# Attention of layer 2 in groups of four query blocks, with the causal mask and the row maximum in one VectorE operation

## The chip, the cores and the metric

The kernel runs on one core of a Trainium2 chip. The metric is the time of one execution on the device, in microseconds; a kernel's time is the median of its runs. The engines are named as in the profile: PE is TensorE (PEld its weight loads), DVE VectorE, ACT ScalarE, POOL GpSimd, and SP issues the DMAs.

## What is computed

The reference is a decoder trunk of two layers over 1024 tokens of width 1024. Layer 1 has a stick-breaking attention and a sliding-window attention side by side, layer 2 a multi-head latent attention with 16 heads; each is followed by a SwiGLU feed-forward part, and norms stand ahead of every part. The change lies in the attention of layer 2:

```python
def one_block(args):
    qn_blk, qr_blk, i = args
    s = (jnp.einsum('bqhd,bshd->bhqs', qn_blk, k_nope, preferred_element_type=F32)
         + jnp.einsum('bqhr,bsr->bhqs', qr_blk, k_rope, preferred_element_type=F32)) * scale
    q_pos = i * BLOCK + jnp.arange(BLOCK)
    s = jnp.where(key_pos[None, :] <= q_pos[:, None], s, -jnp.inf)
    p = jax.nn.softmax(s, axis=-1)
    return jnp.einsum('bhqs,bshd->bqhd', p.astype(v.dtype), v)
```

A head has 64 + 32 features for queries and keys (plain and rotary) and 64 for values. Queries attend to themselves and to all earlier tokens.

## The kernel before

**Tiling.** Tokens lie in reverse order, in eight blocks of 128; so query block b attends to the key blocks b to 7, and block b itself is the diagonal one, with a triangular mask. A head has 36 pairs of a query and a key block. Every product that needs more than one pass of TensorE takes its operands as a high and a low part (`hi`, `lo`): scores take three matmuls (high by high, high by low, low by high), and the product of weights and values (PV) takes two, one for each part of the transposed weights, against values that hold both of their parts side by side.

**Order of work.** The 16 heads are worked in 8 pairs p. `steps(p)` gives a list of steps, each with a `score` and a `pv` half, and `drive` strings the steps of all pairs together: the scores of a step are emitted ahead of the previous step's PV, and the projections of the next pair (queries, keys, values: six items and one of DMAs) are spread as filler over the gaps between a pair's steps. The kernel is built under a planner which then fixes the order on each engine from the dependences and its own estimate of times, so instructions of neighbouring steps are mixed.

**A step** is a head h and a pair c of query blocks (2c and 2c + 1), eight steps per head pair. The order is c = 3, 2, 1, 0 for each head; in pair 0 both heads do c = 3, 2 first, since the projections of that pair are done one token half after the other.

**Scores** (L1257 to L1294). A row of a query block is n = 1024 - 128 b wide. It is cut into one or two parts (`cuts`), the diagonal part first; each part goes to a PSUM bank `z`, of which there are three. The three matmuls stand at L1277. For the first part a fourth matmul (L1280), identity by `maskb` in bf16, adds the mask. VectorE takes the negated maximum of each part (L1283), and, where there are two parts, the smaller of the two (L1286). ScalarE then computes Exp with that as its bias (L1290) into a tile `w` and the row's sum. `w` is a ring of four tiles of 1024 columns, which were the trigonometric tables of the rotary part before.

**PV** (`pv`, L347 to L377). Two key blocks by two query blocks are transposed by TensorE into one PSUM bank `t` of 512 columns (L361); where a key block lies ahead of a query block, zeros are put there by a bf16 matmul (L359). ScalarE copies the high part (`pth`, L364), VectorE subtracts to get the low one (`ptl`, L365), and two matmuls of 256 columns per key block accumulate into a PSUM bank `mm` (L369). At the end ScalarE copies half of the rows (L374) and VectorE adds them to the other half into the output tile of a token half (L376). There are three banks for `t`, two for `mm`; the projections use `mm` too.

**After a token half** of a head pair, `normalise` turns the sums into reciprocals, brings them through DRAM to all partitions and multiplies on POOL, and `spill` writes both parts of the result to DRAM.

Of the kernel before, what the change touches and what calls it, by code (L numbers as in the profile page):

```python
# [10 lines left out]
F32 = mybir.dt.float32  # L11
# [9 lines left out]
P = 128  # L21
# [42 lines left out]
class Kernel:  # L64
# [19 lines left out]
    def tl(self, pool, shape, dt, tag, bufs=1):  # L84
        """A tile of a pool, or the next one of the tag's ring."""
# [18 lines left out]
    def consts(self):  # L104
# [4 lines left out]
        self.identb = self.tl(cp, [P, P], BF16, "identb")  # L109
# [12 lines left out]
        self.maskb = self.tl(cp, [P, 2, P], BF16, "maskb")  # L122
        nc.gpsimd.memset(self.maskb, 0.0)
        for i, op in enumerate((ALU.is_gt, ALU.is_ge)):
            nc.gpsimd.affine_select(
                out=self.maskb[:, i, :], in_=self.maskb[:, i, :], pattern=[[1, P]],
                compare_op=op, fill=NEG, base=0, channel_multiplier=-1)
# [18 lines left out]
    def stream(self, units):  # L146
        """Weight units in the order of their use, each loaded one use ahead."""
# [85 lines left out]
    def stat_acc(self, accs, src, k):  # L233
        """Sums of squares: even terms on one engine, odd ones on another."""
# [48 lines left out]
    def spill(self, k, hf, o):  # L283
        """Both parts of a finished head pair to DRAM, where the output projection fetches them."""
# [7 lines left out]
    def normalise(self, sums, hf, o, tag, bufs):  # L292
        """o, rows by head pair and columns by query, over the sums [query, (head, block)] of its rows."""
# [258 lines left out]
    def sb_steps(self, p, boxes, done):  # L552
# [4 lines left out]
        def score(h, c):  # L557
# [5 lines left out]
            for qi in range(2):  # L563
# [4 lines left out]
                for w in cuts:  # L568
# [8 lines left out]
                    if prev is None:  # L577
                        nc.tensor.matmul(z[:, ext:ext + P], self.identb, self.maskb[:, 0, :], start=False, stop=True)
# [946 lines left out]
```

## Time and profile before

| | us |
|---|---|
| median of three runs | 2531.31 (2531.25 to 2532.11) |
| span of the profiled execution | 2526.1 |
| first scores of layer 2 | 1329.65 |
| last PV matmul of layer 2 | 1730.25 |
| granted clock, mean over the span | 0.976 |

The span is the time from the first to the last instruction of one execution that was profiled; the median is of other runs, without a profile, and holds what lies around the span too. The profile gives busy time per engine and per group of instructions, the idle time ahead of a group with what ended it, and the granted clock of TensorE. The chain of work that ended last covers only the last few per cent of the span, so the middle of the kernel is read from stretches of time and from groups by line.

### The profile page before, as it was taken

What the parts mean: (1) busy time and instruction counts of PE and PEld (TensorE: products, weight loads), DVE (VectorE), ACT (ScalarE), POOL (GpSimd) and SP (SyncE); (2) the same over time, 40 slices, a digit from 0 to 9 for tenths busy, and PEclk for the clock granted to TensorE, in tenths of its full rate; (3) what the DMA queues carried; (4) which work ended last, traced back from release to release, by engine and by line L of the source; (5) the groups of instructions that cost most, each with busy time, mean ns of one, the idle gap of its engine ahead of it and who ended that gap; (6) DMA issues with size and microseconds to landing.
All of it is one profiled execution on the core that took longest, in us unless ns stands there. A gap on an engine that the chain in (4) does not pass through costs nothing. (4 is left out here: it accounts for less than half of the span.)

```text
span 2526.1 us, 34111 instructions
## 1 busy us (share of the span) xinstructions
PE 2365.6 (94%) x11364; PEld 1920.4 (76%) x11364; DVE 1960.4 (78%) x2952; ACT 1272.7 (50%) x2571; POOL 975.6 (39%) x761
## 2 busy tenths in 40 slices
PE   7999899997999999999988999999979999999996
PEld 5777678775888888778766888887758888887784
DVE  6988967668766666898987788885597666678988
ACT  6666656544333333444655787774433333344453
POOL 5322233216965343432222323321064344334333
PEclk9999999988999999999999999999989999999998
DMA  3001115741233224653343111135213233255531
GB/s 122 22 34 43 50 60 178 243 164 42 88 121 121 92 105 148 208 174 105 117 132 101 49 63 60 55 133 191 90 42 113 96 109 108 97 173 178 167 102 70
DMA packets 154445, 275.59 MB, mean 109 GB/s; under 512 B 19260, under 2 KB 27933, under 8 KB 154269
## 3 DMA queue, kind: packets, MB, share of 16 engines
q1 hardware_dynamic: 154268, 273.42, 32.1%
q8 instruction: 89, 1.46, 0.2%
q14 instruction: 88, 0.71, 0.1%
HBM read 197.75 MB, written 75.07 MB: 108 GB/s over the span
## 5 line engine op out<-in xcount | busy, mean ns | idle before, releaser
L139 ACT CAST whi<-wa 128x512 fp32r<-128x512 f32 (+1 forms) x438 | 265.9, 608 | 509.7 <-PE mm L217 128.9
L140 DVE TENSOR_TENSOR wlo<-wa,whi 128x512 fp32r<-128x512 f32 (+1 forms) x438 | 332.1, 759 | 70.7 <-ACT whi L139 70.2
L170 POOL TENSOR_TENSOR wa<-s,wa 128x512 f32<-128x512 f32 (+1 forms) x64 | 96.8, 1512 | 357.2 <-DVE wlo L140 330.5
L365 DVE TENSOR_TENSOR ptl<-t,pth 128x512 fp32r<-128x512 f32 x240 | 161.9, 681 | 15.5 <-ACT pth L364 14.4
L140 DVE TENSOR_TENSOR wlo<-wb,whi 128x512 fp32r<-128x512 f32 (+1 forms) x128 | 134.2, 1048 | 38.6 <-ACT whi L139 38.4
L199 POOL TENSOR_TENSOR s<-wb,wb 128x512 f32<-128x512 f32 (+1 forms) x64 | 106.6, 1666 | 144.9 <-DVE wlo L140 136.5
L1277 PE MATMUL z<-mk,mq 128*128 128x512 f32 (+2 forms) x576 | 147.3, 366 | 10.4 <-ACT w L1290 9.7
L361 PE MATMUL t<-ident,w 128*128 128x128 f32 x864 | 145.1, 281 | 10.2 <-DVE ptl L365 6.6
L364 ACT CAST pth<-t 128x512 fp32r<-128x512 f32 x240 | 137.5, 593 | 23.7 <-PE t L361 13.6
L139 ACT CAST whi<-wb 128x512 fp32r<-128x512 f32 (+1 forms) x128 | 77.5, 605 | 139.6 <-PE d L217 44.3
L369 PE MATMUL mm<-pth,v 128*128 128x256 f32 x480 | 140.1, 309 | 4.0 <-ACT pth L364 2.7
L369 PE MATMUL mm<-ptl,v 128*128 128x256 f32 x480 | 132.3, 300 | 9.1 <-DVE ptl L365 8.8
L216 PE MATMUL mm<-hh,whi 128*128 128x512 f32 x312 | 126.3, 405 | 4.8 <-DVE ev L424 2.8
L1290 ACT ACTIVATE w<-z,st 128x512 f32<-128x512 f32 (+3 forms) x192 | 110.6, 582 | 32.8 <-DVE st L1286 23.5
L1283 DVE TENSOR_REDUCE st<-z 128x1 f32<-128x512 f32 (+1 forms) x192 | 104.3, 549 | 27.2 <-PE z L1277 19.1
L218 PE MATMUL mm<-hh,wlo 128*128 128x512 f32 x312 | 122.8, 394 | 0.0
L217 PE MATMUL mm<-hl,whi 128*128 128x512 f32 x312 | 122.7, 393 | 0.0
L170 POOL TENSOR_TENSOR wa<-wa,wa 128x512 f32<-128x512 f32 (+1 forms) x64 | 93.2, 1457 | 66.3 <-issue 52.9
L770 POOL TENSOR_TENSOR c<-c,c 128x512 f32<-128x512 f32 x60 | 91.6, 1539 | 68.9 <-DVE c L865 67.3
L361 PEld LDWEIGHTS t<-ident,w 128*128 128x128 f32 x864 | 103.3, 144 | 18.9 <-DVE ptl L365 7.7
L170 POOL TENSOR_TENSOR wb<-wa,wb 128x512 f32<-128x512 f32 (+1 forms) x64 | 97.4, 1522 | 42.4 <-DMA wa<-w_gate 35.6
L1277 PEld LDWEIGHTS z<-mk,mq 128*128 128x128 f32 x576 | 92.5, 192 | 23.7 <-ACT w L1290 14.9
(507 smaller groups left out, 7532.2 us busy)
## 6 DMA issues: line engine op xcount, KB each, us to landing
ld<-a SPq DMA_DIRECT2D x158, 256.0 KB, 3.7
a<-c SPq DMA_DIRECT2D x120, 256.0 KB, 2.1
wa<-w_gate SPq DMA_DIRECT2D x56, 256.0 KB, 2.6
wa<-w_up SPq DMA_DIRECT2D x56, 256.0 KB, 2.6
wb<-w_gate SPq DMA_DIRECT2D x40, 256.0 KB, 2.8
wb<-w_up SPq DMA_DIRECT2D x40, 256.0 KB, 2.7
wa<-w_in SPq DMA_DIRECT2D x36, 256.0 KB, 2.6
wa<-w_out SPq DMA_DIRECT2D x32, 256.0 KB, 3.5
```

The source lines that it names most:

```text
L139: nc.scalar.copy(hi[:, :n], raw[:, :n])
L140: nc.vector.tensor_tensor(lo[:, :n], raw[:, :n], f(hi[:, :n]), ALU.subtract)
L170: sub = lambda o, x, y: nc.gpsimd.tensor_tensor(o, x, y, ALU.subtract)
L216: mm(ps, wh, xh, start=first, stop=False)
L217: mm(ps, wh, xl, start=False, stop=False)
L218: mm(ps, wl, xh, start=False, stop=last)
L361: nc.tensor.transpose(dst, blocks(qi, kk), self.ident)
L364: nc.scalar.copy(hi, t)
L365: nc.vector.tensor_tensor(lo, t, f(hi), ALU.subtract)
L369: nc.tensor.matmul(o[:, :256], vs, pt[:, j * 256:(j + 1) * 256], start=(kb == kb0 and j == 0 and i == 0), stop=(kb == NB - 2 and j == 1 an ...
L1277: nc.tensor.matmul(z[:, :wd + ext], qq[:, q0:q0 + P], kk[:, k0 - ext:k0 + wd], start=y == 0, stop=y == 2 and x > 0)
L1290: nc.scalar.activation(w[:, o:o + wd], zs[x], AF.Exp, bias=st[:, 2 * np_ - 2:2 * np_ - 1], accum_out=box[p]["s"][c // 2][:, 8 * x + j:8 * ...
```

## The change

Scores and PV of layer 2 go by a head h and a group g of four query blocks, so a head pair has four steps: (h, 1), (h, 0) for each head, for all pairs alike. PV is a new function, which takes one key block by up to four query blocks to a `t` bank: a key block that all four queries attend to makes one part of 512 columns, the next one is 384 wide, and the last two share a part of 512. `pv` stays in use in layer 1.

```diff
+    def pv4(self, g, ws, v, h, ot):
+        nc = self.nc
+        k0 = 4 * g
+        full = [[(kb, 4)] for kb in range(NB - 1, k0 + 2, -1)]
+        o = self.bank("mm")
+        for part in full + [[(k0 + 2, 3)], [(k0 + 1, 2), (k0, 2)]]:
+            t = self.bank("t")
+            n = 0
+            for kb, nq in part:
+                for i in range(nq):
+                    dst = t[:, n:n + P]
+                    kk = kb - k0 - i
+                    if kk < 0:
+                        nc.tensor.matmul(dst, self.zerob, self.zerob, start=True, stop=True)
+                    else:
+                        nc.tensor.transpose(dst, ws[i][:, kk * P:(kk + 1) * P], self.ident)
+                    n += P
+            hi = self.tl(self.atp, [P, HALF], F32R, "pth", self.npt)
+            lo = self.tl(self.atp, [P, HALF], F32R, "ptl", self.npt)
+            nc.scalar.copy(hi[:, :n], t[:, :n])
+            nc.vector.tensor_tensor(lo[:, :n], t[:, :n], f(hi[:, :n]), ALU.subtract)
+            c = 0
+            for kb, nq in part:
+                vs = v[:, kb, h, :, :].rearrange("p a d -> p (a d)")
+                for i, pt in enumerate((hi, lo)):
+                    nc.tensor.matmul(o[:, :nq * P], vs, pt[:, c:c + nq * P],
+                                     start=kb == NB - 1 and i == 0, stop=kb == k0 and i == 1)
+                c += nq * P
+        m0, l0 = (0, 64) if h == 0 else (64, 0)
+        tmp = self.tl(self.atp, [P, HALF], F32, "otmp", 1)
+        nc.scalar.copy(tmp[m0:m0 + 64, :], o[l0:l0 + 64, :])
+        nc.vector.tensor_tensor(ot[m0:m0 + 64, :], o[m0:m0 + 64, :], tmp[m0:m0 + 64, :], ALU.add)
```

In the scores the far part of a row comes first, then the diagonal one. No matmul adds the mask. VectorE adds it in `tensor_tensor_reduce`, which also negates, writes the result back over the scores in PSUM, and takes the minimum, starting from the far part's negated maximum where there is one. Exp of the diagonal part then has the scale -1.

```diff
-                    for x, wd in enumerate(cuts):
-                        z = self.bank("z")
-                        ext = P if wd == P else 0
-                        for y, (qq, kk) in enumerate(passes):
-                            nc.tensor.matmul(z[:, :wd + ext], qq[:, q0:q0 + P], kk[:, k0 - ext:k0 + wd],
-                                             start=y == 0, stop=y == 2 and x > 0)
-                        if x == 0:
-                            nc.tensor.matmul(z[:, ext:ext + P], self.identb, self.maskb[:, 1, :],
-                                             start=False, stop=True)
-                        zs.append(z[:, ext:ext + wd])
-                        nc.vector.tensor_reduce(st[:, x:x + 1], zs[x], AX.X, ALU.max, negate=True)
-                        k0 += wd
-                    if np_ == 2:
-                        nc.vector.tensor_tensor(st[:, 2:3], st[:, 0:1], st[:, 1:2], ALU.min)
+                    for x in range(len(cuts))[::-1]:
+                        wd = cuts[x]
+                        o -= wd
+                        z = self.bank("z")
+                        ext = P if wd == P else 0
+                        for y, (qq, kk) in enumerate(passes):
+                            nc.tensor.matmul(z[:, :wd + ext], qq[:, q0:q0 + P], kk[:, q0 + o - ext:q0 + o + wd],
+                                             start=y == 0, stop=y == 2)
+                        zz = z[:, ext:ext + wd]
+                        if x == 1:
+                            nc.vector.tensor_reduce(st[:, :1], zz, AX.X, ALU.max, negate=True)
+                            far = zz
+                        else:
+                            nc.vector.tensor_tensor_reduce(
+                                zz, zz, mask[:, :wd], scale=-1.0, scalar=st[:, :1] if len(cuts) == 2 else big,
+                                op0=ALU.add, op1=ALU.min, accum_out=st[:, 1:])
+                            nc.scalar.activation(w[:, :wd], zz, AF.Exp, bias=st[:, 1:], scale=-1.0,
+                                                 accum_out=box[p]["s"][g][:, j:j + 1])
+                    if len(cuts) == 2:
+                        nc.scalar.activation(w[:, cuts[0]:], far, AF.Exp, bias=st[:, 1:],
+                                             accum_out=box[p]["s"][g][:, 8 + j:9 + j])
```

The tiles: the four blocks of group 0 use the first columns of the four `w` tiles, those of group 1 a new tile `w4` and the last columns of three of the four. The mask is a new tile [128, 512] in bf16, triangular in its first 128 columns and zero in the others, made by two POOL operations once the last pool of the mixer is open. `otmp` is one tile of 512 columns in place of two of 256.

```diff
-        rings["w"] = trig + tab
+        w = trig + tab
+        wt = [w, [new(pool, "w4")] + [w[3 - i][:, S - (3 - i) * P:] for i in range(3)]]
+        mask = self.causal(new(pool, "mask", dt=BF16), ALU.is_ge)
...
-        rings["otmp"] = [t[0][:, :256], t[0][:, 256:]]
+        rings["otmp"] = t
...
-        orders = [[(h, c) for g in ((3, 2), (1, 0)) for h in range(2) for c in g] if p == 0 else
-                  [(h, c) for h in range(2) for c in (3, 2, 1, 0)] for p in range(8)]
+        order = [(h, g) for h in range(2) for g in (1, 0)]
+        big = 3e38
```

The identity in bf16 and the mask of layer 1, which were constants of the whole kernel, are now tiles of the attention of layer 1, with the same values and uses there; `causal` is the function that makes a mask. Docstrings and comments are taken out, which changes no instruction.

More of the change, by code (lines that the diff above doesn't have):

```diff
@@ L121, in consts, with causal @@
         nc.vector.memset(self.log_q, math.log(QSCALE))
[L122 to L127, printed above, removed]
+    def causal(self, mask, op):
+        self.nc.gpsimd.memset(mask, 0.0)
+        self.nc.gpsimd.affine_select(out=mask[:, :P], in_=mask[:, :P], pattern=[[1, P]], compare_op=op,
+                                     fill=NEG, base=0, channel_multiplier=-1)
+        return mask
     def load_half(self, src, n):
@@ L577, in score @@
                     if prev is None:
-                        nc.tensor.matmul(z[:, ext:ext + P], self.identb, self.maskb[:, 0, :], start=False, stop=True)
+                        nc.tensor.matmul(z[:, ext:ext + P], self.identb, self.maskb, start=False, stop=True)
                     nc.scalar.activation(u[:, :w], zz, AF.Sigmoid, scale=-0.125)
@@ L609, in layer0_attention @@
             self.sinks = self.tl(self.atp, [P, 8], F32, "sinks")
+            self.identb = self.tl(self.atp, [P, P], BF16, "identb")
+            self.maskb = self.causal(self.tl(self.atp, [P, P], BF16, "maskb"), ALU.is_gt)
             def xsrc(k, hf):
@@ L1249, in second @@
                     nc.sync.dma_start(out=f(kt[h][1][x][r:r + 32, :]), in_=f(kt[h][0][x][r:r + 32, :]))
-        orders = [[(h, c) for g in ((3, 2), (1, 0)) for h in range(2) for c in g] if p == 0 else
-                  [(h, c) for h in range(2) for c in (3, 2, 1, 0)] for p in range(8)]
+        order = [(h, g) for h in range(2) for g in (1, 0)]
+        big = 3e38
         def steps(p):
-            s, order = p % 2, orders[p]
+            s = p % 2
             def score(i):
-                h, c = order[i]
+                h, g = order[i]
                 if i == 0:
@@ L1264, in score @@
                 ws = []
-                for qi in range(2):
-                    qb = 2 * c + qi
-                    q0 = qb * P
+                for qi in range(4):
+                    q0 = (4 * g + qi) * P
                     n = S - q0
                     cuts = {P: [P], 5 * P: [2 * P, 3 * P]}.get(n) or ([n] if n <= HALF else [HALF, n - HALF])
-                    np_ = len(cuts)
-                    st = self.tl(pool, [P, 3], F32, "st", 8)
-                    zs, k0 = [], q0
-                    for x, wd in enumerate(cuts):
+                    st = self.tl(pool, [P, 2], F32, "st", 8)
+                    w = wt[g][qi][:, :n]
+                    j = 4 * h + qi
+                    o = n
+                    for x in range(len(cuts))[::-1]:
+                        wd = cuts[x]
+                        o -= wd
                         z = self.bank("z")
@@ L1293, in score @@
+                    if len(cuts) == 2:
+                        nc.scalar.activation(w[:, cuts[0]:], far, AF.Exp, bias=st[:, 1:],
+                                             accum_out=box[p]["s"][g][:, 8 + j:9 + j])
                     ws.append(w)
-                return lambda qi, kk: ws[qi][:, kk * P:(kk + 1) * P]
+                return ws
             def pv(i, cur):
-                h, c = order[i]
-                self.pv(c, cur, box[p]["v"], h, box[p]["o"])
-                if i == max(j for j in range(8) if order[j][1] // 2 == c // 2):
-                    hf = c // 2
+                h, hf = order[i]
@@ L1301, in pv @@
+                self.pv4(hf, cur, box[p]["v"], h, box[p]["o"][hf])
+                if i == max(j for j in range(4) if order[j][1] == hf):
                     s, o = box[p]["s"][hf], box[p]["o"][hf]
@@ L1308, in pv @@
                         self.spill(p, hf, o)
-            return [(lambda i=i: score(i), lambda cur, i=i: pv(i, cur)) for i in range(8)]
+            return [(lambda i=i: score(i), lambda cur, i=i: pv(i, cur)) for i in range(4)]
         oact = [[None, None] for _ in range(NT)]
```

7 lines of the change are left out of this document (removed).

## The prediction

> **What bounds the kernel now.** I read the head of the page first, then the busy time by stretch over the attention of layer 2, then the groups by line in it, then single rows.
>
> ```profile
> span 2526.1 us, 34111 instructions
> PE 2365.6 (94%) x11364; PEld 1920.4 (76%) x11364; DVE 1960.4 (78%) x2952; ACT 1272.7 (50%) x2571; POOL 975.6 (39%) x761
> ```
>
> The runs have a median of 2531.31 us, so 5.2 us lie around the profiled span; I keep those and work on the span. PE is the busiest engine over the whole, but only the attention of layer 2 is touched. In the windows view (length, then PE, PEld, DVE, ACT, POOL busy, granted clock, DMA share, GB/s):
>
> ```profile
> 1345.00:1385.00 40.00, 29.01 (x135) 22.24 (x134) 32.63 (x58) 22.07 (x50) 5.89 (x6) 0.87 0.39 119
> 1385.00:1700.00 315.00, 310.96 (x2070) 267.51 (x2069) 260.77 (x517) 250.48 (x646) 105.56 (x82) 1.00 0.20 67
> ```
>
> From 1385 to 1700 PE is busy 311 of 315 us, DVE 261 (83%), ACT 250 (80%), and DMA is no limit. So a microsecond taken off PE there is a microsecond of the kernel, and DVE or ACT time counts only where PE waits for it. At the start (1345 to 1385) PE has 11 us idle and DVE is the fuller engine.
>
> Matmuls overlap, so their durations (0.28 us for a 256-wide one) are not their price; the distance between starts is. From the timeline of PE (start, duration):
>
> ```profile
> 1387.87 0.28 PE L369 MATMUL mm<-pth,v 128*128 128x256 f32 x1
> 1387.99 0.28 PE L369 MATMUL mm<-ptl,v 128*128 128x256 f32 x1
> ...
> 1388.58 0.86 PE L1277 MATMUL z<-mk,mq 128*128 128x512 f32 x3
> 1389.28 0.23 PE L1280 MATMUL z<-maskb,identb 128*128 128x128 bf16 x1
> 1389.34 0.60 PE L361 MATMUL t<-ident,w 128*128 128x128 f32 x4
> ...
> 1391.85 0.69 PE L1277 MATMUL z<-mk,mq 128*128 128x384 f32 x3
> 1392.38 0.27 PE L361 MATMUL t<-ident,w 128*128 128x128 f32 x1
> 1392.49 0.22 PE L359 MATMUL t<-zerob 128*128 128x128 bf16 x1
> 1392.55 0.28 PE L361 MATMUL t<-ident,w 128*128 128x128 f32 x1
> ```
>
> A 256-wide matmul takes 0.12 us of PE, a 512-wide one 0.70 / 3 = 0.23, a 384-wide one 0.53 / 3 = 0.177, a transpose 0.11, a mask matmul (L1280) or a zero matmul (L359) 0.06. The price goes with the columns: two 256-wide matmuls cost what one 512-wide costs. That decides most of what follows.
>
> **The change, part by part.** The groups that it touches:
>
> ```profile
> L369 PE MATMUL mm<-pth,v 128*128 128x256 f32 x320 | 93.5, 308 | 1.7 <-ACT pth L364 1.4
> L369 PE MATMUL mm<-ptl,v 128*128 128x256 f32 x320 | 87.4, 297 | 1.3 <-DVE ptl L365 1.2
> L1280 PE MATMUL z<-maskb,identb 128*128 128x128 bf16 x128 | 29.7, 232 | 0.0
> L359 PE MATMUL t<-zerob 128*128 128x128 bf16 x64 | 14.2, 222 | 0.0
> L365 DVE TENSOR_TENSOR ptl<-t,pth 128x512 fp32r<-128x512 f32 x160 | 108.0, 683 | 13.6 <-ACT pth L364 12.9
> L1283 DVE TENSOR_REDUCE st<-z 128x1 f32<-128x512 f32 x80 | 54.7, 684 | 15.6 <-PE z L1277 9.1 <-PE z L1280 5.9
> L1286 DVE TENSOR_TENSOR st<-st 128x1 f32<-128x1 f32 x64 | 28.8, 450 | 0.9
> ```
>
> *PV in groups of four.* For each of 16 heads the group of blocks 4 to 7 goes through three evictions (512, 384, 512 wide) and the group 0 to 3 through seven (512 five times, 384, 512). The 36 transposes stay. The 40 matmuls of 256 become 12 of 512, 4 of 384 and 8 of 256, and the four zero blocks become two. PE over 16 heads: 640 x 0.117 = 74.9 us becomes 192 x 0.229 + 64 x 0.173 + 128 x 0.117 = 70.0 us (the paces to the last digit are medians of the rows of which one each is shown), so **-4.9 us**; zero matmuls 32 x 0.056 = **-1.8 us**. The wide form itself gives nothing: the saving is the 512 columns per head that were padding. Evictions: 32 of 160 narrow from 512 to 384, some 4 us each on ACT and DVE, and half as many copies and additions at the end of a group (L374, L376), each twice as wide; neither is on PE's path.
>
> *The mask.* 128 mask matmuls go: 128 x 0.056 = **-7.2 us** of PE. On DVE the maximum of the diagonal part becomes one operation with two inputs (scores in PSUM, mask in SBUF) that also writes the masked scores back to PSUM. The trace has no such operation. Its price at 512 wide lies between the plain maximum that it replaces (684 ns) and the dearest DVE form of that width, the scan of layer 1; the nearest row is L365, also one PSUM and one SBUF input, 512 wide:
>
> ```profile
> L365 DVE TENSOR_TENSOR ptl<-t,pth x240: 654/681/693, 72.0 to 1729.2; 128x512 fp32r<-128x512 f32 x120
> L581 DVE TENSOR_TENSOR_SCAN u<-u 128x512 f32<-128x512 f32 x32 | 42.8, 1338 | 4.2 <-ACT u L579 4.1
> L1286 DVE TENSOR_TENSOR st<-st x64: 142/162/1259, 1378.5 to 1724.1; 128x1 f32<-128x1 f32 x64
> 1498.80 1.28 POOL L306 TENSOR_TENSOR acc<-acc,sq 128x512 f32<-128x512 f32 x1
> 1499.67 0.41 DVE L1286 TENSOR_TENSOR st<-st 128x1 f32<-128x1 f32 x1
> ```
>
> I take 0.70 us, near L365: about nothing above the reduction. At the scan's price the 128 operations, on average 384 wide, would add 128 x 0.65 x 0.75 = 63 us to DVE. A page of the Trainium skill speaks against the change here: "VectorE: DVE Perf Modes", section "Two Vector instructions with no wait between them", says that an operation which also writes out its accumulator is two instructions, the main one and a read of the accumulator. No run here shows it on DVE; with the 162 ns of the smallest DVE rows as an estimate it would be 21 us of DVE, less than the minima below give back.
>
> *The minimum of two maxima* (L1286) goes, since the second operation starts from the first one's result: -28.8 us of DVE, and, more to the point, a link of 450 ns in the chain that ends in Exp and frees the score banks. Its median is only 162 ns; the long ones, like the row at 1499.67, end together with a POOL operation (1498.80 + 1.28 = 1500.08). The new operation has one SBUF input, like L365, whose longest of 240 is 693 ns, so it should not be held that way.
>
> *What the shorter chain is worth on PE.* From the waits between 1345 and 1725 (total, times, longest):
>
> ```profile
> ACT w L1290 <- DVE st L1286: 23.5, 31, 1.9
> PEld z L1277 <- ACT w L1290: 14.9, 22, 3.9
> PE z L1277 <- ACT w L1290: 9.7, 10, 3.5
> 1354.98 0.37 ACT L1290 ACTIVATE w<-z,st 128x128 f32<-128x128 f32 x1 [2.64 <-DVE w L1141]
> 1355.50 0.93 PE L1277 MATMUL z<-mk,mq 128*128 128x384 f32 x3 [3.48 <-ACT w L1290]
> 1368.49 0.98 PE L1277 MATMUL z<-mk,mq 128*128 128x512 f32 x3 [2.56 <-ACT w L1290]
> ```
>
> PE waits for a score bank 14.9 us by its weight loads, 9.7 by its matmuls, the same stalls seen twice. The two longest, 3.48 and 2.56 us, lie at the start; with the shorter ones there I count some 8 us of the 14.9 to the start and 7 to the steady part. Of the 7 I take **-3 us**. The far part now comes first and its Exp last, so its bank is held longer while the diagonal one is freed sooner; that is why not all goes.
>
> *The start.* The Exps of the first head wait until 1354.98 for L1141, because w lies in the trigonometric tables, and PE waits 3.48 us behind them. Now the first group writes w4, which is new, and columns 640 and up of the other tiles, which belong to the token half done first. That half's columns are not held back if dependences go by region, and they do:
>
> ```profile
> 1329.65 0.52 PE L1277 MATMUL z<-mk,mq 128*128 128x256 f32 x3
> 1336.25 2.85 POOL L1339 TENSOR_TENSOR mk<-ev,mk 64x512 fp32r<-64x512 f32 x2 [6.44 <-ACT mk L1338]
> ```
>
> Scores read mk before the other half of it is written. So the first PV can fill that gap, while DVE stays the fuller engine (32.6 of 40 us, the rotary products). Against it, pair 0 now takes the second head's early blocks after the first head's late ones. Between nothing and the 8 us I take **-3 us**. The mask's two POOL operations and the moved constants of layer 1 fall where POOL is mostly idle (5.89 of 40 us) and cost nothing; without that cover they delay the first maximum by their own 1 to 2 us, once.
>
> *Larger steps.* There are four steps per head pair in place of eight; the fill items (projections) lie in three gaps, and a group holds its "mm" bank longer, so a projection behind it on that bank waits with PE behind it. No DMA is added; the normalisation keeps its three on SP and moves with the end of its group. The sharpest point is the score step of group 0, 26 blocks, beside the 10-block PV:
>
> ```profile
> L1338 ACT CAST mq<-ev 64x512 fp32r<-64x512 f32 x32 | 19.8, 619 | 9.0 <-DVE ev L1173 8.6
> 1500.45 0.69 ACT L1290 ACTIVATE w<-z,st 128x512 f32<-128x512 f32 x1
> 1501.12 0.58 ACT L1290 ACTIVATE w<-z,st 128x384 f32<-128x384 f32 x1
> 1501.67 0.59 ACT L364 CAST pth<-t 128x512 fp32r<-128x512 f32 x1
> 1714.89 0.79 PE L1277 MATMUL z<-mk,mq 128*128 128x384 f32 x3 [0.37 <-ACT w L1290]
> ```
>
> Exps follow each other at 0.67 us (512 wide) and 0.55 (384); 0.45 for 256 continues the line. ACT needs 4 x 0.67 + 2 x 0.55 + 2 x 0.45 = 4.7 us for the scores, 2.2 for three evictions and a copy at some 0.55, 1.8 for a projection (two of L1338) and its weights: 8.7 us. PE, by the paces above, needs 4.5 for scores, 2.4 for PV with its transposes and 2.1 for nine 512-wide matmuls of the projection: 9.0 us. ACT at 97% of PE, where the fullest step before (15 blocks beside 11) had, counted in the same way, 5.9 of 7.3 us (81%). So PE will wait: I take 0.25 us, near the 0.37 of the row at 1714.89, in each of 16 such steps, **+4 us**; the ends are nothing and 1.5 us each.
>
> **Sum:** -4.9 - 1.8 - 7.2 - 3 - 3 + 4 = -15.9 us: span 2510, time **2515 us**, own range 2506 to 2524.
>
> **Rivals.** *Relief in full* (0.15): the larger steps cost nothing and all score-bank waits go, -13.9 - 7 - 8 = -29, 2502 us. For it: DVE falls from 83% to some 74%. Against: ACT is unchanged at 80% and becomes what frees the banks.
> *Weight loads set PE's pace* (0.03): 256 fewer loads at the 0.117 us distance are -30 us in place of -4.9, 2490 us. Against: a 128-wide transpose with its load takes 0.11, so loads can go faster, and 512-wide matmuls take 0.23. The Trainium skill's "Perfetto Trace Analysis", section "Identifying the Most-Contended Engine", judges TensorE's headroom by weight-load busy time and not by matmul busy time; here that is 267.5 of 315, 85%, and by the distances it is not the limit.
> *The new DVE operation is dear* (0.15): at the scan's price DVE nets +63 - 29 us, 92% of the stage; the chain to Exp is as long as before, and PE's waits for ptl and score banks grow by some 10 us: -13.9 + 4 + 8 = -2, 2529 us. No change, then.
> *Slower* (0.17): ACT bounds the 26-block step. Three score banks let PE run no further ahead, and the projection behind the long-held "mm" bank is not there to fill in, so PE waits 1.5 us in each of the 16: -13.9 + 24 = +10, 2541 us. It decides once the wait per step passes 0.9 us (13.9 / 16). For it: the 97%. Against: in the trace such waits are 0.2 to 0.4 us and the order mixes work of neighbouring steps.
>
> **How the numbers follow.** Forecast 0.50, the rest as given. The measurement can tell 0.2% (5 us) from no change. Faster: 0.50 + 0.15 + 0.03 = 0.68; within: 0.15; slower: 0.17. The range leaves out the slower case and the weight loads (0.20): 2500 to 2533.
>
> **What would show it.** 384 PV matmuls, 512-wide at 0.23 us, no bf16 mask rows, 32 zero rows. The new DVE operation near 0.70 us at 512 wide; at 1.3 us the third rival is near. Waits of PE for w below 14.9 us in total mean relief; above 25 us, clustered in the 26-block steps, the slower case. The forecast fails if PE's busy share from 1385 on falls well below 98%.

## The result, and the profile after

| | before | after |
|---|---|---|
| median, us (six runs each) | 2531.71 (2528.53 to 2533.39) | 2539.36 (2535.45 to 2540.44) |
| ratio | 1 | 1.0032 [1.002, 1.0045] |
| span of the profiled execution | 2526.1 | 2533.7 |

The kernel became 8 us slower. The forecast was 2515 us. The time lies 6 us above the range of 2500 to 2533, and within 2 us of what the slower rival gave (2541).

The head of the page of the kernel after:

```profile
span 2533.7 us, 33322 instructions
PE 2354.0 (93%) x10948; PEld 1904.1 (75%) x10948; DVE 1944.2 (77%) x2984; ACT 1265.7 (50%) x2539; POOL 970.5 (38%) x762
```

PE, DVE and ACT all have less to do than before (PE 11.6 us, DVE 16.2, ACT 7.0), and the span is 7.6 us longer. So no engine got dearer work; what grew is waiting. The windows view of the kernel after (length, then PE, PEld, DVE, ACT, POOL busy, granted clock, DMA share, GB/s) says where:

```profile
1345.00:1385.00 40.00, 27.54 (x117) 21.10 (x117) 31.70 (x64) 20.96 (x48) 5.75 (x7) 0.87 0.39 120
1385.00:1700.00 315.00, 291.14 (x1648) 243.29 (x1647) 239.13 (x529) 236.39 (x600) 106.26 (x82) 0.99 0.19 58
```

In the steady part PE was busy 311 of 315 us and is now busy 291 (92%), while DVE and ACT are busy 76% and 75%. Nobody is full. That is the sign which the prediction named for its failure.

The ends of the head pairs in time (the transposes of a pair's sums) put it in one place. The first pair ends at 1419.8 us before and 1419.6 after. The next six take 273.8 us before and 285.1 after, that is 45.6 and 47.5 us each: 11.3 us lost. The last pair, the only one without projections of a next one, takes 36.7 us to its last PV before and 32.3 after: 4.4 us gained. What follows it takes 795.9 and 796.7 us. So the six pairs that carry projections lose, and the one that carries none gains.

The new and changed operations, from the groups by line of the kernel after (count | busy us, mean ns | idle before):

```profile
L405 PE MATMUL mm<-pth,v 128*128 128x512 f32 x96 | 41.2, 429 | 10.6 <-ACT pth L399 10.3
L405 PE MATMUL mm<-ptl,v 128*128 128x512 f32 x96 | 40.7, 424 | 0.7 <-DVE ptl L400 0.6
...
L1324 DVE CUSTOM_DVE_ANT_0 z<-z,mask,st 128x512 f32<-128x512 f32 x48 | 36.2, 754 | 20.3 <-PE z L1317 14.3 <-ACT pth L399 4.2 <-ACT sq L410 1.7
...
L1324 DVE DVE_READ_ACCUMULATOR2_ANT st<- 128x1 f32 x128 | 17.8, 139 | 0.0
```

All of this is as foreseen or near it: 192 wide PV matmuls, and a mask operation of 0.75 us. It comes with a second instruction of 139 ns that reads the accumulator, as the Trainium skill's "VectorE: DVE Perf Modes", section "Two Vector instructions with no wait between them", has it; the trace agrees, at 139 ns where the prediction estimated 162. The price of the new operation is not where the time went.

The waits of PE in the steady part, 1385 to 1690 us (total, times, longest), first before, then after:

```profile
PEld z L1277 <- ACT w L1290: 3.5, 14, 0.6
...
PE z L1277 <- ACT w L1290: 0.7, 3, 0.3
```

```profile
PEld z L1317 <- ACT w L1327: 18.7, 27, 1.6
PE z L1317 <- ACT w L1327: 12.0, 21, 1.3
...
PE mm L405 <- ACT pth L399: 6.3, 3, 2.1
```

Waits of scores for a free bank went from 0.7 to 12.0 us by the matmuls, and PE now waits 6.3 us in PV for the copy of the transposed weights. One of its three cases, from the timeline of the kernel after (start, duration, engine, line):

```profile
1549.71 1.28 POOL L306 TENSOR_TENSOR acc<-acc,sq 128x512 f32<-128x512 f32 x1
...
1549.89 1.66 DVE L140 TENSOR_TENSOR wlo<-wa,whi 128x512 fp32r<-128x512 f32 x1
...
1551.47 0.41 DVE L345 TENSOR_TENSOR v<-t,v 128x256 fp32r<-128x256 f32 x1
...
1551.92 0.37 ACT L344 CAST v<-t 128x256 fp32r<-128x256 f32 x1 [1.89 <-DVE v L345]
...
1552.97 0.60 ACT L399 CAST pth<-t 128x512 fp32r<-128x512 f32 x1
...
1553.62 0.51 PE L405 MATMUL mm<-pth,v 128*128 128x512 f32 x1 [2.09 <-ACT pth L399]
```

Read it from the bottom. PE waits 2.09 us for `pth`. ACT could have copied it, but in ACT's order the value copies of a projection (L344) stand ahead of it, and the first one shown waited 1.89 us for DVE (L345), which had been busy with a weight split (L140) that took 1.66 us in place of its median 0.69. The projection of the next pair, meant to fill PE's gaps, is here what PE waits behind, and PE has no other projection left to work on: the pair's last projection matmul starts at 1548.78 us, the next pair's first at 1567.10.

### The profile page after: what moved, and what is told of

Read it like the earlier page. It is cut to its first block, busy times and chain, and to the rows that moved or that the text cites. A ratio compares the mean times of both kernels' runs of the same rounds, so it can differ in the third digit from the quotient of the medians.

```text
span 2533.7 us, 33322 instructions
## 1 busy us (share of the span) xinstructions
PE 2354.0 (93%) x10948; PEld 1904.1 (75%) x10948; DVE 1944.2 (77%) x2984; ACT 1265.7 (50%) x2539; POOL 970.5 (38%) x762
## 5 line engine op out<-in xcount | busy, mean ns | idle before, releaser
L140 DVE TENSOR_TENSOR wlo<-wa,whi 128x512 fp32r<-128x512 f32 (+1 forms) x438 | 337.8, 772 | 73.6 <-ACT whi L139 71.0
L140 DVE TENSOR_TENSOR wlo<-wb,whi 128x512 fp32r<-128x512 f32 (+1 forms) x128 | 132.6, 1036 | 38.5 <-ACT whi L139 38.4
L199 POOL TENSOR_TENSOR s<-wb,wb 128x512 f32<-128x512 f32 (+1 forms) x64 | 100.9, 1577 | 145.1 <-DVE wlo L140 136.3
L400 DVE TENSOR_TENSOR ptl<-t,pth 128x512 fp32r<-128x512 f32 (+1 forms) x160 | 102.9, 659 | 22.0 <-ACT pth L399 21.2
L399 ACT CAST pth<-t 128x512 fp32r<-128x512 f32 (+1 forms) x160 | 86.9, 570 | 24.0 <-PE t L395 20.4
L395 PE MATMUL t<-ident,w 128*128 128x128 f32 x576 | 92.4, 274 | 1.6 <-ACT w L1330 1.6
L750 POOL TENSOR_TENSOR acc<-acc,sq 128x512 f32<-128x512 f32 x26 | 35.7, 1373 | 140.0 <-ACT sq L745 140.0
L1327 ACT ACTIVATE w<-z,st 128x512 f32<-128x512 f32 (+3 forms) x128 | 75.4, 594 | 24.0 <-DVE st L1324 21.5
L395 PEld LDWEIGHTS t<-ident,w 128*128 128x128 f32 x576 | 72.4, 141 | 12.9 <-ACT w L1330 1.8
L405 PE MATMUL mm<-pth,v 128*128 128x512 f32 (+1 forms) x192 | 71.5, 374 | 10.6 <-ACT pth L399 10.3
L139 ACT CAST whi<-s 128x512 fp32r<-128x512 f32 (+1 forms) x64 | 38.7, 605 | 71.4 <-PE b L217 28.6
```

The lines of the kernel that those rows point to most:

```text
L139: nc.scalar.copy(hi[:, :n], raw[:, :n])
L140: nc.vector.tensor_tensor(lo[:, :n], raw[:, :n], f(hi[:, :n]), ALU.subtract)
L199: nc.gpsimd.tensor_tensor(s1, a21, a22, ALU.add)
L395: nc.tensor.transpose(dst, ws[i][:, kk * P:(kk + 1) * P], self.ident)
L400: nc.vector.tensor_tensor(lo[:, :n], t[:, :n], f(hi[:, :n]), ALU.subtract)
L405: nc.tensor.matmul(o[:, :nq * P], vs, pt[:, c:c + nq * P], start=kb == NB - 1 and i == 0, stop=kb == k0 and i == 1)
```

## The experiments

Each ratio is to the kernel before, for the variants on the same chip, with its 95% interval; 0.1% is 2.5 us. "A pair" below is the time between the ends of two head pairs, read as above, in the mean over the six pairs with projections. Each variant goes through the planner, so the order on each engine is worked out anew. A letter stands for a theory within the runs of one round; where it isn't spelled out, the text below says in words what was at stake. This table holds the runs that vary the parts of the change against one another. "Apart" means one projection item of the next pair at a time; "gathered" means three gaps of 2, 2 and 3 items, as the changed kernel has them.

| scores and PV | mask by matmul, minimum of its own | mask and maximum in one operation |
|---|---|---|
| steps of two blocks, PV by pairs, apart | before: 1 | e1: 0.9981 [0.9973, 0.9990] |
| steps of two blocks, PV by pairs, gathered | e12: 1.0113 [1.0093, 1.0134] | |
| steps of four, PV by pairs, gathered | e11: 1.0125 [1.0106, 1.0144] | e10: 1.0026 [1.0017, 1.0035] |
| steps of four, PV in groups, gathered | e2: 1.0117 [1.0103, 1.0131] | after: 1.0032 [1.0020, 1.0045] |
| half steps, PV in groups, gathered | | e9: 1.0037 [1.0023, 1.0052] |
| half steps, PV in groups, apart | e7: 1.0031 [1.0020, 1.0042] | e4: 0.9950 [0.9936, 0.9963] |
| scores by four, PV in groups, apart | | e13: 0.9960 [0.9948, 0.9972] |

### The two parts alone: e1_mask_only, e2_group_only

e1 is the kernel before with the mask operation in its score half, nothing else. e2 is the kernel after with the scores, mask matmul, maxima and minimum of before:

```diff
-                        if x == 1:
-                            nc.vector.tensor_reduce(st[:, :1], zz, AX.X, ALU.max, negate=True)
-                            far = zz
-                        else:
-                            nc.vector.tensor_tensor_reduce(
...
+                        if x == 0:
+                            nc.tensor.matmul(z[:, ext:ext + P], self.identb2, mask[:, :P],
+                                             start=False, stop=True)
+                        zs.append(z[:, ext:ext + wd])
+                        nc.vector.tensor_reduce(st[:, x:x + 1], zs[x], AX.X, ALU.max, negate=True)
+                        k0 += wd
+                    if np_ == 2:
+                        nc.vector.tensor_tensor(st[:, 2:3], st[:, 0:1], st[:, 1:2], ALU.min)
```

> The kernel before with the mask part of the change alone: mask and row maximum in one VectorE operation, PV by pairs of query blocks, eight steps per head pair. Theory A (the grouping costs, the mask part gains): TensorE loses 128 mask matmuls (7.2 us) and one link of the chain to Exp; the time is 2520 to 2526 us against 2531.5, and a head pair takes 44.5 to 45 us against 45.6 before. Rival B (the new VectorE operation costs): the time is 2531 us or more, with VectorE rows of 754 ns and 139 ns for the accumulator in the chain and waits of PE for w above 15 us.

> The changed kernel with the scores, mask matmul and maxima of before: only the grouping by four query blocks is new. Theory A: worse than the changed kernel, about 2539 + 7 to 10 = 2546 to 2549 us, a head pair takes 48.5 to 49.5 us against 47.5. Rival B: better than the changed kernel, 2525 to 2530 us, since 6.7 us of PE columns and zero blocks are gone and nothing else costs.

Measured: e1 2524.46 us, 0.9981; e2 2559.24 us, 1.0117. The mask part gives 5 us beside PV by pairs. The groups cost 30 us alone and 13 beside the mask part. So the loss belongs to the groups, more of it than either theory for e2 had, and the two parts don't add up.

The time of e1 is as theory A had it, but a pair is not: it takes 46.0 us, where 44.5 to 45 were expected and the kernel before takes 45.6. PE is busy 43.7 us in it in place of 45.1. Over the six pairs 8 us of PE went, and they got 1.9 us longer; the gain lies in the first and the last pair (2.8 and 3.0 us) and in what follows the last PV (2.0), which the edit doesn't touch. What PE got free it spent waiting for score banks (1385 to 1690 us, against 0.7 us before):

```profile
PE z L1285 <- ACT w L1295: 7.4, 14, 0.7
...
PE z L1285 <- ACT w L1298: 1.4, 5, 0.3
```

### Projections over four gaps: e3_fill_spread

The kernel after, with the items in all four gaps of a head pair (2, 2, 2, 1) in place of three:

```diff
+            if n == 4 and len(filler) in (7, 8):
+                cut = [0, len(filler) - 5, len(filler) - 3, len(filler) - 1, len(filler)]
+                for i in range(4):
+                    fill[len(steps) + i] = filler[cut[i]:cut[i + 1]]
```

> The changed kernel with the fill items over four gaps (2, 2, 2, 1) in place of three (2, 2, 3), so that the last three projections of a pair do not stand together. Theory A1 (the cluster of k, v, v makes the 2.25 us stall of every second pair, where PV waits for pth behind value copies): the stall goes, 3 times 2.25 us and some of the 1.5 us stalls, the time is 2528 to 2534 us. Theory A2 (ACT and the score banks bound the 26-block step, whatever stands in the gaps): unchanged, 2537 to 2541 us.

Measured: 2529.34 us, 0.9997 [0.9988, 1.0006]. Against the kernel after that is 9 us back, by an edit that changes no arithmetic and no instruction's size.

### Half steps: e4_half_steps, e9_half_coarse_fill, e13_full_scores_spread

e4 emits the same work in halves: two rows of scores, half a PV, and at most one projection half (rotary items go with the first) after it. Scores run two half steps ahead.

```diff
+        for x in range(2):
+            allsteps[x][0]()
+        for x, (_, pv) in enumerate(allsteps):
+            if x + 2 < len(allsteps):
+                allsteps[x + 2][0]()
+            pv()
+            for fn in fill.get(x, ()):
+                fn()
```

> The changed kernel, its groups of four and its new VectorE operation, but emitted in half steps: two rows of scores, half of a PV, at most one projection, in turns, with scores two half steps ahead. If the size of the steps in the emitted order is what costs (theory A in both forms), the gain forecast comes back: 2514 to 2524 us, and a head pair takes 43.5 to 45 us. If it is the longer held mm bank or the planner's own order, it stays at 2535 us or above.

Measured: 2517.01 us (2515.56 to 2517.57), 0.9950 [0.9936, 0.9963]: 21 us below the kernel after and 13 below the one before. But e4 changes two things, the size of a step and the spread of the projections. e9 takes the spread back:

```diff
-                filler = [filler[:2]] + [[x] for x in filler[2:]]
...
+            for x in range(3):
+                fill[len(allsteps) + 2 * x + 1] = filler[x * len(filler) // 3:(x + 1) * len(filler) // 3]
```

> The half steps of e4_half_steps, but the projections in three gaps of a head pair (2, 2 and 3 items after half steps 1, 3 and 5), as the changed kernel has them. Theory S (the size of a step is what costs: 26 blocks of scores emitted ahead of one PV): the time stays with e4_half_steps, 2512 to 2522 us. Theory F (the gathered projections cost, and the half steps helped only by spreading them): it goes back to 2528 to 2540 us. Spreading alone gave 10 us in full steps, so near 2527 us would be half and half.

Measured: 2539.98 us, 1.0037. All of the gain is gone, so the half steps by themselves are worth nothing. e13 is the other corner, e4 with the scores of a whole step emitted together again:

```diff
-            if x + 2 < len(allsteps):
-                allsteps[x + 2][0]()
+            for y in (x + 2, x + 3):
+                if x % 2 == 0 and y < len(allsteps):
+                    allsteps[y][0]()
```

> e4_half_steps with its projections one by one between the halves of a PV, but the scores of a whole step (10 or 26 blocks) emitted together ahead of the previous PV, as the changed kernel has them. Theory F: the score step does not matter, 2513 to 2522 us. Theory S: 2528 to 2540 us, as the changed kernel.

Measured: 2517.82 us, 0.9960. The 26-block score step stands there as in the kernel after, and costs nothing. What costs is that the projections come together.

### Gathering in the kernel before: e12_before_gathered

If that is so, the kernel before must lose in the same way when only its projections are gathered:

```diff
+            if n == 8 and len(filler) in (7, 8):
+                for i in range(3):
+                    fill[len(steps) + 2 * i + 1] = filler[i * len(filler) // 3:(i + 1) * len(filler) // 3]
+                steps += seg
+                continue
```

> The kernel before, unchanged in its steps, scores, mask and PV, but with the projections of the next pair in three gaps of a head pair (2, 2 and 3 items, after steps 1, 3 and 5) in place of one item after each step. Theory F (gathered projections are the cost): 2545 to 2562 us, as e11_wide_steps. Theory S (the larger score step is): 2526 to 2534 us.

Measured: 2555.63 us, 1.0113 [1.0093, 1.0134], 28 us more with the same instructions. One head pair cut in eight equal stretches shows how. First before (whole pair 45.6 us; columns as above), then e12 (49.0 us):

```profile
1516.60:1522.30 5.70, 5.70 (x39) 4.94 (x38) 5.52 (x10) 4.24 (x10) 2.37 (x2) 1.00 0.26 95
...
1533.70:1539.40 5.70, 5.29 (x36) 4.44 (x35) 4.79 (x10) 4.13 (x11) 2.26 (x2) 1.00 0.02 5
1539.40:1545.10 5.70, 5.57 (x33) 4.47 (x32) 4.50 (x9) 3.96 (x11) 3.28 (x3) 1.00 0.16 46
```

```profile
1527.40:1533.50 6.10, 5.93 (x45) 5.16 (x43) 5.15 (x11) 5.06 (x16) 0.49 (x1) 1.00 0.12 44
1533.50:1539.70 6.20, 6.20 (x43) 5.44 (x43) 5.28 (x10) 4.71 (x11) 2.42 (x3) 1.00 0.24 87
1539.70:1545.80 6.10, 5.29 (x36) 4.29 (x35) 4.64 (x10) 5.17 (x16) 2.21 (x2) 1.00 0.14 43
1545.80:1551.90 6.10, 6.10 (x44) 5.31 (x42) 4.37 (x9) 3.44 (x7) 2.57 (x2) 1.00 0.14 44
1551.90:1558.00 6.10, 4.77 (x34) 4.06 (x33) 3.80 (x11) 5.25 (x14) 2.54 (x2) 1.00 0.01 3
1558.00:1564.20 6.20, 6.07 (x28) 4.58 (x27) 4.87 (x8) 3.77 (x11) 3.14 (x3) 1.00 0.22 67
1564.20:1570.30 6.10, 4.60 (x35) 3.73 (x34) 5.51 (x14) 4.50 (x15) 2.48 (x2) 1.00 0.45 145
1570.30:1576.40 6.10, 6.10 (x53) 5.67 (x51) 5.00 (x12) 4.67 (x11) 0.00 (x0) 1.00 0.00 2
```

The same stretches of e12 for the evictions of finished projections alone (DVE's share in `ev`, six of 0.69 us in a pair):

```profile
1533.50:1539.70 6.20, 0.69 (x1) 1.00 0.24 87
...
1545.80:1551.90 6.10, 1.37 (x2) 1.00 0.14 44
1551.90:1558.00 6.10, 0.02 (x1) 1.00 0.01 3
1558.00:1564.20 6.20, 1.95 (x3) 1.00 0.22 67
1564.20:1570.30 6.10, 0.12 (x1) 1.00 0.45 145
```

Before, the two lower rows of the three shown are the only stretches of the eight in which PE is idle at all, 0.5 us together. In e12 PE is full, or nearly, where a projection is finished (6.20, 6.10, 6.07) and has 0.8, 1.3 and 1.5 us idle in the stretch behind each, 3.9 us in the whole pair. That is 3.4 more than before, and the pair is 3.4 us longer. A projection is six or nine matmuls of 512 columns, and no wait of PE stands ahead of any of them in e12, so PE always has work beside it. Scores and PV wait for ACT and DVE at every bank: in the steady part PE waits 20.2 us for score banks, where it was 0.7 before. My reading is that one projection beside each of them keeps PE going, and that two or three together leave stretches where the chain through DVE and ACT sets the pace. ACT has least to do beside two projections (3.44 of 6.10 us) and DVE in the stretch behind them (3.80 of 6.10).

### PV by pairs in the large steps: e10_wide_steps_mask, e11_wide_steps

Both keep steps of four blocks with gathered projections, and go back to `pv` in two calls; e10 with the mask operation, e11 without:

```diff
-                self.pv4(hf, cur, box[p]["v"], h, box[p]["o"][hf])
+                for c in (2 * hf + 1, 2 * hf):
+                    self.pv(c, lambda qi, kk: cur[2 * (c % 2) + qi][:, kk * P:(kk + 1) * P],
+                            box[p]["v"], h, box[p]["o"])
```

> The changed kernel with its steps of four query blocks and its mask operation, but PV by pairs (two calls per step, 256 columns, four zero blocks per head and group, as before). Theory S (the size of the step): about e1_mask_only plus the 21 us that larger steps cost elsewhere, 2540 to 2550 us. Theory G (the wide PV with its long-held mm bank needs small steps; with PV by pairs a larger step costs nothing): near e1_mask_only, 2522 to 2530 us, so faster than the changed kernel in spite of 5 to 7 us more of PE.

> The kernel before with steps of four query blocks and nothing else of the change: PV by pairs, mask by matmul, maxima as before. Theory S: the kernel before plus some 21 us, 2545 to 2560 us. Theory G: no change, 2526 to 2535 us; then the loss of e2_group_only (28 us) lies in the wide PV and not in the order of steps.

Measured: e10 2537.15 us, 1.0026; e11 2562.15 us, 1.0125. The first lies between the ranges of both theories. Set beside the kernel after (1.0032) and e2 (1.0117), the wide PV changes the time by +1.5 and -2 us, both within the intervals: nothing, though by the paces in the prediction it takes 6.7 us off PE. But all four have gathered projections, and PE is busy at most 286 of the 305 us from 1385 to 1690 in them. What the wide PV is worth where PE is full was not measured alone: with projections apart the groups come with other steps, and they gain 5 (e13) and 8 us (e4) against e1 with the mask operation, and lose 8 us (e7) without it. e11 and e12 agree (1.0125 and 1.0113): in the kernel before, larger steps cost no more than gathered projections do alone.

### Order of the two Exps and a fourth score bank: e5, e6, e8

With PE waiting for score banks, the far part's bank, which is now freed last, was a suspect. e5 is the kernel after and e6 is e4, each with the far part's Exp first:

```diff
-                            nc.scalar.activation(w[:, :wd], zz, AF.Exp, bias=st[:, 1:], scale=-1.0,
-                                                 accum_out=box[p]["s"][g][:, j:j + 1])
+                            near = zz
...
+                    nc.scalar.activation(w[:, :cuts[0]], near, AF.Exp, bias=st[:, 1:], scale=-1.0,
+                                         accum_out=box[p]["s"][g][:, j:j + 1])
```

> The changed kernel with the two Exps of a row exchanged: the far part first, then the diagonal one. In the traces a score bank of the far part is held 6.6 us from its first matmul to the end of its Exp, one of the diagonal part 3.6 us, 4.6 in the mean, against 4.7 before the change, and the banks go round in a ring, so that the bank needed next is the far one. Theory Z (score banks that come free out of turn make the waits of PE for w): the far hold falls by 0.7 to 1 us, PE's waits for w (12.0 us by matmuls from 1385 to 1690) fall to below 8, the time is 2530 to 2535 us. Rival: only the emitted order counts, so unchanged, 2537 to 2541 us.

> The half-step kernel (2517 us) with the two Exps of a row exchanged, far part first. By theory Z a little faster, 2513 to 2517 us, since its waits for w are only 2.5 us already; by the rival 2516 to 2519 us.

Measured: e5 2538.71 us, 1.0038 [1.0025, 1.0050], no change; e6 2524.26 us, 0.9985 [0.9976, 0.9994], 9 us worse than e4. Freeing the far bank sooner helps nowhere. e8 is the kernel after with four score banks and two transpose banks:

```diff
-self.nbank = {"mm": 2, "t": 3, "z": 3}
+self.nbank = {"mm": 2, "t": 2, "z": 4}
```

> The changed kernel with four banks for scores and two for transposes in place of three and three. Theory Z: PE's waits for w shrink to below half, and the time falls to 2530 to 2536 us unless the transposes' eviction, with a bank less, takes it back (then waits of PE for pth and ptl or of transposes show it). Rival (ACT's total work bounds the big step): waits for w stay, 2537 us or more.

Measured: 2569.16 us, 1.0161 [1.0148, 1.0175]. PE's waits in its steady part:

```profile
PE z L1317 <- ACT w L1327: 17.0, 17, 2.3
PEld mm L405 <- DVE ptl L400: 14.6, 39, 0.6
```

One bank more and the waits for banks went up, from 12.0 to 17.0 us, with new ones behind the low part of the transposed weights. The transposes lost a bank at the same time, so the run doesn't price a score bank by itself; but the named releaser of a wait was not its cure.

### What the mask part is worth: e7, e14, e15, e16

e7 is e4 with scores, mask matmul, maxima and minimum of before (the diff of e2, in half steps).

> The half-step kernel with scores, mask matmul and maxima as before the change: the grouping alone, in small steps. If the wide PV gains its PE columns and zero blocks (6.7 us) once the steps are small, and the mask part another 7 to 8 us, this is 2523 to 2527 us. If the mask part gains 20 us beside groups of four whatever the steps, it is 2535 to 2540 us.

Measured: 2534.70 us, 1.0031. The mask part is worth 20 us there, and 21 between e2 and the kernel after, against 5 between before and e1. Its matmuls are 7.2 us of PE. e14 is e7 without them, so without the causal mask; e15 is e4 with as many matmuls of zeros put back:

```diff
+                        if x == 0:
+                            nc.tensor.matmul(z[:, ext:ext + P], self.zerob, self.zerob, start=False, stop=True)
```

> e7_half_no_mask without its 128 mask matmuls: the causal mask on the diagonal blocks is left out of the computation; the maxima, their minimum and the order of the parts stay. Theory P (the mask part gives what it takes off PE): 128 x 0.056 = 7 us below e7_half_no_mask's ratio, about 2527 us, and the rest of the 18 us between e7_half_no_mask and e4_half_steps lies in the minimum that goes and in the order of the parts. Theory Q (the mask matmuls, which must follow their bank's three, hold the score chain too): nearly all 18 us, 2517 to 2521 us.

> e4_half_steps with 128 bf16 matmuls of zeros put where the mask matmuls stood, the mask and maximum still in one DVE operation. Theory P: 7 us more than e4_half_steps, some 2522 to 2526 us. Theory Q: near e7_half_no_mask, 2530 to 2537 us.

Measured: e14 2533.36 us, 1.0022 [1.0011, 1.0033], 2 us from e7; e15 2516.62 us, 0.9956 [0.9941, 0.9972], 1.5 us from e4. Both theories miss the times: over the whole kernel the 7.2 us of PE are not seen. The steady part (1385 to 1690 us) of e4, the same of e15, and e15's group of the matmuls put back:

```profile
1385.00:1690.00 305.00, 294.31 (x1702) 250.72 (x1702) 237.25 (x546) 239.27 (x620) 101.97 (x79) 0.98 0.21 69
```

```profile
1385.00:1690.00 305.00, 302.07 (x1823) 246.92 (x1822) 239.93 (x548) 239.13 (x622) 100.31 (x78) 1.00 0.22 72
```

```profile
L1325 PE MATMUL z<-zerob 128*128 128x128 bf16 x128 | 29.4, 229 | 0.0
```

PE is 99% busy in e15 and 96% in e4, at the same time for the kernel. By itself this looks as if the added 7.8 us of busy time had gone into slack, but the pairs show otherwise. Two neighbouring pairs of e4, then 4 us of the first of them, then the same two pairs of e15 (windows view as above):

```profile
1462.93:1508.84 45.91, 43.67 (x251) 37.56 (x249) 34.78 (x80) 35.85 (x93) 15.79 (x12) 0.96 0.18 57
1508.84:1551.88 43.04, 42.08 (x249) 35.84 (x248) 34.34 (x79) 34.32 (x89) 15.46 (x12) 1.00 0.20 62
1502.90:1504.90 2.00, 2.00 (x11) 1.83 (x10) 0.72 (x2) 1.60 (x5) 1.28 (x1) 0.55 0.35 131
1504.90:1506.90 2.00, 2.00 (x8) 1.61 (x7) 0.69 (x1) 0.83 (x2) 0.00 (x0) 0.59 0.35 131
```

```profile
1462.48:1506.28 43.80, 43.67 (x265) 35.91 (x264) 34.70 (x79) 34.86 (x91) 15.44 (x12) 1.00 0.19 60
1506.28:1550.07 43.79, 43.67 (x265) 35.91 (x264) 34.67 (x79) 34.84 (x91) 15.43 (x12) 1.00 0.19 61
```

Every second pair of e4 is some 3 us longer. PE waits there once for 1.8 or 1.9 us (PV for `ptl`), and in the 4 us behind that wait the granted clock lies between 0.50 and 0.67. The other three take 42.7 to 43.0 us. In e15, whose order was worked out anew, no pair has such a wait, the clock is 1.00 from 1385 to 1690, and the six take 43.8 to 44.4 us. That is 1.2 us more in the mean than the three undisturbed pairs of e4, where 16 matmuls at 0.056 are 0.9. So the zeros cost about their price, and what hides it is the 9 us that e4 loses in its other three pairs. e14 and e7 agree: the six pairs take 270.5 us without the mask matmuls and 275.5 with them, 5.0 us less, where 96 at 0.056 are 5.4. The rest of e14 took 3.6 us longer in the profiled executions, so little of it is left in the time of the kernel.

e16 is e4 with the minimum alone back, as a DVE operation of its own; mask operation, order of the parts and absence of mask matmuls stay:

```diff
-                                zz, zz, mask[:, :wd], scale=-1.0, scalar=st[:, :1] if len(cuts) == 2 else big,
-                                op0=ALU.add, op1=ALU.min, accum_out=st[:, 1:])
+                                zz, zz, mask[:, :wd], scale=-1.0, scalar=big,
+                                op0=ALU.add, op1=ALU.min, accum_out=st[:, 1:2])
+                            b = st[:, 1:2]
+                            if len(cuts) == 2:
+                                b = st[:, 2:3]
+                                nc.vector.tensor_tensor(b, st[:, 0:1], st[:, 1:2], ALU.min)
```

> e4_half_steps with the minimum of two maxima back as a DVE operation of its own: the mask operation starts from a constant, and 64 small operations take the smaller of the two. No mask matmul. Theory M (the minimum as a link between DVE and Exp, held by POOL at times, is what the mask part is worth): near e14_half_no_mask_matmul, 2528 to 2535 us. Theory O (the order of the parts, far part first and diagonal Exp first, is what it is worth): near e4_half_steps, 2515 to 2520 us.

Measured: 2538.01 us, 1.0043 [1.0029, 1.0056]: 23 us more than e4, from 64 small operations. Their rows in e16 (from the groups, then min/median/max of their durations):

```profile
L1335 DVE TENSOR_TENSOR st<-st 128x1 f32<-128x1 f32 x64 | 21.4, 335 | 0.5
```

```profile
L1335 DVE TENSOR_TENSOR st<-st x64: 140/158/1189, 1373.5 to 1727.9; 128x1 f32<-128x1 f32 x64
```

They take 21.4 us of DVE, twice what 64 of the median would (10.1), so half of it lies in long ones; and each stands between the last maximum and the first Exp of its row. In half steps beside groups, all of the mask part's worth over the whole kernel is this operation. Whether it costs by its own time, by the long ones or by what the planner puts around it was not told apart; nor why it costs 20 us beside PV in groups and only 5 beside PV by pairs.

## Why the prediction was wrong

**"So a microsecond taken off PE there is a microsecond of the kernel": this step failed.** It was read from 311 busy of 315 us. The terms that rest on it, -4.9 and -1.8 us for the wide PV and -7.2 us for the mask matmuls, were sized rightly as work (192 wide matmuls, no mask row), but work taken off PE became waiting. In the kernel after, PE is busy 20 us less in that part and the time rose. In e1, which differs from the kernel before in the mask part alone, 8 us went off PE over six pairs, and these got 1.9 us longer, with 8.8 us of waits for score banks in place of 0.7. With gathered projections the wide PV gave nothing (e10 and e11 against their partners). In half steps it went the other way: the six pairs of e14 gave 5.0 of 5.4 us. So what a microsecond of PE is worth was not to be read from the busy share. The prediction itself noted that the durations of matmuls overlap and are not their price, and then took the busy share made of the same durations as a bound.

**"Larger steps, +4 us": this step failed in size, and in what it looked at, and it turned the sign.** It counted ACT against PE in the 26-block step. e13 keeps that step and is fast. The three gaps of the projections stood in the same paragraph, with no price. They cost 28 us in the kernel before (e12), and with the mask operation 22 us in half steps (e9 against e4, which differ in nothing else), 18 us between the kernel after and e13, and 11 us between e10 and e1.

**"Shorter chain, -3 us": a term that was too small, and its reason unsound.** The waits for banks of which 7 us were put to the steady part were 3.5 us there by the weight loads, and 0.7 by the matmuls; the rest lay at the start. They rose instead of falling, to 18.7 and 12.0 in the kernel after. The gathered projections are not the whole reason: in e1, where they stay apart, the waits by the matmuls rose to 8.8. The minimum, which is the link that went, was worth 23 us beside groups in half steps (e16). Of the 5 us of e1 beside pairs its share was not measured.

**"The start, -3 us": nothing is seen.** The first pair ends 0.2 us sooner in the kernel after and 0.2 us later in e4, which has its projections apart.

**The new DVE operation** was priced rightly: 754 ns against the 0.70 us taken, plus 139 ns for the accumulator's read. By line, those that start from the far part's maximum (min/median/max in ns):

```profile
L1324 DVE CUSTOM_DVE_ANT_0 z<-z,mask,st x64: 471/750/760, 1372.1 to 1728.3; 128x512 f32<-128x512 f32 x48, 128x256 f32<-128x256 f32 x16
```

The longest is 760 ns. None ran long as the old minimum did, and that was expected of an operation with only one input in SBUF.

**The slower rival** had the direction, and the size to 2 us. Of its mechanism one clause held, that the projection is not there to fill in. "ACT bounds the 26-block step" did not, and three score banks were not shown to be the limit. So the agreement in size is luck. Its chance of 0.17 came from pricing the clause that was wrong.

**The sum by the runs**: before to e1, -0.19% (the mask part); e1 to e10, +0.45% (steps of four with gathered projections); e10 to the kernel after, +0.06% (the wide PV). Together +0.32%, or 8 us. With the projections spread, the groups and the mask operation give -0.50% (e4), 2517 us, close to the forecast's time but not by its sum: 5 us by the mask part (e1) where it had 10, 8 by the groups (e4 against e1) where it had 7, and nothing at the start. Without the mask part the same groups cost 8 us (e7), so such parts can't be priced one by one and added.

## What to carry to other kernels

When a loop's steps get larger, look first at what was spread over its gaps: work that waits for nobody is worth most when every stretch of dependent work has a piece of it alongside. A busy share near 100% does not show that time on that engine is time of the kernel: take some work off or put some back, and see whether the same stretch gets shorter or longer. Compare stretch by stretch, not only the time of the kernel; where each variant gets an order of its own, as here, a stall that comes or goes elsewhere can hide the answer (e15). And a small operation on the chain between engines can weigh more than many matmuls on the busiest one (e16).

## What was not expected of the hardware

The weight split of the stall above has both inputs in SBUF, and its durations in the kernel after spread widely (min/median/max in ns):

```profile
L140 DVE TENSOR_TENSOR wlo<-wa,whi x438: 542/685/1775, 4.6 to 2498.2; 128x512 fp32r<-128x512 f32 x130, 128x384 fp32r<-128x384 f32 x16
```

The one at 1549.89 us took 1.66 us and ended 0.56 us after the POOL operation beside it (1549.71 + 1.28); the minimum of e16, 128x1, took 158 ns in the median and 1189 at most. Rows of that kind ran long beside POOL and rows with a PSUM input didn't; that POOL is the cause was only argued from such rows.

The mask operation is cheaper where it starts from a constant and not from a column of a tile, 690 against 754 ns at 512 wide:

```profile
L1324 DVE CUSTOM_DVE_ANT_0 z<-z,mask 128x512 f32<-128x512 f32 x16 | 11.0, 690 | 0.0
```
